# Two of three expert-key tiles beside the value tiles are multiplied as split halves, from a ring of three buffers

## The chip, the core and the metric

The kernel runs on one core of one Trainium2 chip. The metric is the device time of the program in microseconds (us); lower is better. Three runs of the kernel before gave 1677.07, 1669.07 and 1673.76 us, so its median is 1673.76 us. The engines are named as in the profile: PE multiplies matrices (PEld is its weight load), DVE, ACT and POOL work on elements, SP issues transfers.

## The reference

One decoder layer on 512 tokens of width 1024. Three token mixers (forgetting attention, windowed attention, attention to a memory) come first. The change lies in the second half, a product-key layer of 16384 single-neuron experts:

```python
def peer_ffn(h, w_q, keys1, keys2, u, v):
    ...                       # per token: 8 heads x 16 experts by product keys, softmax gates
    def chunk(args):
        h_c, e_c, g_c = args
        a = jnp.einsum('cd,ced->ce', h_c.astype(jnp.float32), u[e_c].astype(jnp.float32))
        act = jax.nn.gelu(a, approximate=False) * g_c
        return jnp.einsum('ce,ced->cd', act, v[e_c].astype(jnp.float32))
```

`u` and `v` are 16384 x 1024 in float32, 64 MB each. A token uses 128 of the 16384 experts.

## The kernel before, in words

The 512 tokens are four blocks of 128. Blocks 0 and 1 take the *row* way: for each of the 128 chosen experts of each token POOL gathers one row of `u` (then of `v`) by an indirect transfer of 128 rows of 4 KB, and DVE multiplies it in (line 819 for `u`, line 828 for `v`). That is 512 row steps; `step()` issues transfers ahead (up to `ahead`, `AHEAD` = 4, `AHEAD + MORE` = 6 for a while) and does one step.

Blocks 2 and 3 (`DENSE`, 256 tokens, `TD`) take the *dense* way: all 16384 experts in 128 tiles of 128.

- `dense_u(k)`: one U tile, 512 KB, comes by SP's queue into a ring of `URING` = 6 buffers (three in the big buffer `hhi`, three in `hlo`). Eight float32 matmuls (line 921, weights: the U tile, moving: `h2f`, the 256 tokens) give the scores; ACT's Gelu puts them into `ga(k)`.
- spreading: `spread(n)` for 64 batches of four tokens turns the gates into a dense layout. Gates of the first 33 tiles are multiplied into `ga` at once, the others go to DRAM (`gd`) and come back later as `gq`, in 512-byte pieces.
- `dense_v(k)`: one V tile, 512 KB. `operands(k)` prepares it: DVE multiplies the gates in from `gq` (line 1036, from k = 33 on), ACT casts the tile to a float32r part `whi` (line 1040), DVE subtracts to get the rest `wlo` (line 125), and `ga(k)` is split likewise into `ah` and `al` (lines 132 and 133). Then `mm3` does three float32r matmuls per piece (lines 137 to 139). Every fourth tile is *whole*: float32 matmuls from a buffer `last`, no split (line 1058).

Splitting a float32 operand into two float32r parts and multiplying three of the four products is `mm3`:

```python
def mm3(ps, l, r, first=True, last=True):
    (lh, ll), (rh, rl) = l, r
    PE.matmul(ps, lh, rh, start=first, stop=False)
    PE.matmul(ps, lh, rl, start=False, stop=False)
    PE.matmul(ps, ll, rh, start=False, stop=last)
```

U runs ahead of V by `LAG` = 57 tiles: U tiles 0 to 57 are done before and during spreading, the other 70 inside the V loop. That loop runs over 128 V tiles; in its turn k stand `operands(k + 1)`, the row steps that are due (about two), the U tile that is due (in 70 of the first 118 turns), and `dense_v(k)`. PE, DVE and POOL execute in the written order (a manual schedule). ACT and SP are put in order by a scheduler. The buffers `raw` (V tiles as they land), `whi` and `wlo` have three slots each; rows may also use `raw` slots while `ahead` is 6. `ah` and `al` have two.

Of the kernel before, what the change touches and what calls it, by code (L numbers as in the profile page):

```python
# [7 lines left out]
F32 = mybir.dt.float32  # L8
F32R = mybir.dt.float32r
# [3 lines left out]
AF = mybir.ActivationFunctionType  # L13
# [3 lines left out]
S, D, NB, KC = 512, 1024, 4, 8  # L17
# [4 lines left out]
NK = 128  # L22
NJ = PH * TOPK
NC = 64
GROUPS = ((0,), (1, 2, 3))
BIG = 3
DENSE = (2, 3)
ND = len(DENSE)
TD = 128 * ND
FIRST_U, COVER, DURING, AFTER = 8, 24, 25, 0  # L30
# [2 lines left out]
BETWEEN, UNWEIGHED, IN_RAW = 12, 14, 0  # L33
LAG = FIRST_U + COVER + DURING + AFTER
GA_LATE = 6
URING = 6
VFAR = 3
GQ_AT, GQ_PARTS = 1, 4
RAW_MORE = 5
STEPS_U = 4  # L40
# [6 lines left out]
WSLOT = 4 * 264  # L47
AHEAD, ROWS_IN, MORE = 4, 5, 2
# [6 lines left out]
def tile_block(ctx: ExitStack, tc: tile.TileContext, t: dict, out: bass.AP):  # L55
    nc = tc.nc
# [12 lines left out]
    def bank(tag):  # L69
        return psum.tile([128, 512], F32, tag=tag, name=tag, bufs=BANKS[tag])  # L70
# [45 lines left out]
    def rest(loaded, pool):  # L116
        raw, hi, n = loaded
        w = raw.shape[1]
        lo = wp.tile([128, WSLOT], F32R, tag="wlo", name="wlo")[:, :w]
        due[0] += pool  # L120
        if due[0] >= 1.0:
            due[0] -= 1.0
            G.tensor_tensor(lo, raw, hi.bitcast(F32), op=OP.subtract)
        else:
            V.tensor_sub(lo, raw, hi.bitcast(F32))  # L125
        return [x.rearrange("p (n w) -> p n w", n=n) for x in (hi, lo)]
# [4 lines left out]
    def split(hi, lo, src):  # L131
        A.copy(hi, src)
        V.tensor_sub(lo, src, hi.bitcast(F32))
# [6 lines that stand above are left out]
# [4 lines left out]
    def wide(tag, nb, dt=F32):  # L144

        slot = big.tile([128, (1 if tag == "mg0" else BIG) * D], dt, tag=tag, name=tag)
        return slot[:, :nb * D]
# [7 lines left out]
    def chunks(x):  # L155

        return [x[:, k] for k in range(x.shape[1])]
# [731 lines left out]
    def ga(k):  # L889
        s = k % (LAG + 1)  # L890
        return soon[:, s] if s <= LAG - GA_LATE else late[0][:, s - (LAG + 1 - GA_LATE)]

    def fetch_u(k):
        if not FIRST_U <= k < NK:
            return
        s = (k - FIRST_U) % URING
        if s % BIG == 0 or not u_ring[s // BIG]:
            if k - FIRST_U < URING:
                u_ring[s // BIG] = by_token(wide(("hhi", "hlo")[s // BIG], BIG))
        u_raw[k] = u_ring[s // BIG][:, s % BIG]  # L900
        nc.sync.dma_start(u_raw[k], t["uT"][k])
# [3 lines left out]
    def fetch_u_to(k):  # L905
        while u_next[0] <= min(k, NK - 1):
            fetch_u(u_next[0])
            u_next[0] += 1

    def dense_u(k):  # L910

        if k < FIRST_U:
            w = load_raw(t["uT"][k], D)[:, :D]
        else:
            fetch_u_to(k + URING - 1)
            w = u_raw.pop(k)
        w = w.rearrange("p (n w) -> p n w", n=KC)
        yield
        ps = bank("mm")
        for dc in range(KC):  # L920
            PE.matmul(ps[:, :TD], w[:, dc], h2f[dc], start=dc == 0, stop=dc == KC - 1)  # L921
            yield
        A.activation(ga(k), ps[:, :TD], AF.Gelu)  # L923
# [48 lines left out]
    def build_sides(n):  # L972
        i, _, ts = tokens(n)
        eT = slots[i]
        o = sp.tile([128, 2, GT, NK], F32, tag="o", name="o", bufs=AHD + 1)
        V.tensor_tensor(o, numbers[:, None, None, :].to_broadcast([128, 2, GT, NK]),
                        eT[:, :2, ts, None].to_broadcast([128, 2, GT, NK]), op=OP.is_equal)
        if n % 4 == 3:
            G.tensor_tensor(o[:, 0], o[:, 0], eT[:, 2, ts, None].to_broadcast([128, GT, NK]), op=OP.mult)
        else:  # L980
            for u in range(GT):
                A.activation(o[:, 0, u], o[:, 0, u], AF.Copy, scale=eT[:, 2, ts.start + u:ts.start + u + 1])
        sides[n] = o
# [35 lines left out]
    def fetch_v(k):  # L1019
        if k < NK:  # L1020
            pool, n = (gp[0], 1) if k % WHOLE == WHOLE - 1 else (wp, None)
            tag = "last" if n else "raw"
            raw = pool.tile([128, D if n else WSLOT], F32, tag=tag, name=tag, **({"bufs": n} if n else {}))
            v_raw[k] = raw[:, :D]
            nc.sync.dma_start(v_raw[k], t["peer_v"][k * NK:(k + 1) * NK])

    def operands(k):

        whole = k % WHOLE == WHOLE - 1
        fetch_v(k + VFAR)  # L1030
        get_gates(k + GK, k % GK - GQ_AT)
        raw, a = v_raw.pop(k), ga(k)
        if k >= KEPT:
            m = gq[k - k % GK][:, :, k % GK]
            g = a.rearrange("p (g t) -> p g t", t=TG)
            V.tensor_mul(g, m, g)
        if whole:
            return whole, [raw], a, a
        hi = wp.tile([128, WSLOT], F32R, tag="whi", name="whi")[:, :D]
        A.copy(hi, raw)  # L1040
        w = [x[:, 0] for x in rest((raw, hi, 1), 0.0)]
        ah = gp[0].tile([128, TD], F32R, tag="ah", name="ah")
        al = gp[0].tile([128, TD], F32R, tag="al", name="al")
        split(ah, al, a)
        return whole, w, ah, al

    def dense_v(k, whole, w, ah, al):
# [14 lines left out]
    NBAT = ND * 128 // GT  # L1062
# [23 lines left out]
    for n in range(AHD, NBAT + AHD):  # L1086
        if n < NBAT:
            build_sides(n)
        credit[0] += STEPS_N
        while credit[0] >= 1.0 and done[0] < known[0]:  # L1090
            credit[0] -= 1.0
            step()
        if (n + 4) % PER == 0 and n + 4 < NBAT:
            turn_block((n + 4) // PER)
        spread(n - AHD)
        for _ in range(STEPS_U):
            if tile_u is None and FIRST_U + COVER + n * DURING // NBAT >= k_u:
                tile_u = dense_u(k_u)
                next(tile_u)
                k_u += 1  # L1100
            elif tile_u is not None and next(tile_u, 1):
                tile_u = None
    for _ in tile_u or ():
        pass
    share[0], ahead[0] = 0.0, AHEAD
    spreading.close()
    gp = [ctx.enter_context(tc.tile_pool(name="gp", bufs=2))]
    while k_u < LAG:
        list(dense_u(k_u))
        k_u += 1  # L1110
    for k in range(VFAR):
        fetch_v(k)
    start, ready = done[0], operands(0)
    for k in range(NK):
        now, ready = ready, operands(k + 1) if k + 1 < NK else None
        while done[0] < min(len(JOBS), start + (len(JOBS) - start) * (k + 1) // (NK - 5)):
            step()
        while k_u < min(NK, LAG + (NK - LAG) * (k + 1) // (NK - 10)):
            list(dense_u(k_u))
            k_u += 1  # L1120
        dense_v(k, *now)
    for b in (0, 1):
        nc.sync.dma_start(out[b * 128:(b + 1) * 128], x1[b])
    for i, b in enumerate(DENSE):
        for hf in range(2):
# [93 lines left out]
```

## Time and profile before

| | |
|---|---|
| runs | 1669.07 to 1677.07 us, median 1673.76 |
| the profiled execution | 1675.4 us; its span, first to last instruction, 1673.5 |
| PE busy | 1583.6 us, 95% |
| DVE / ACT / POOL busy | 1362.9 / 721.9 / 840.7 us |
| memory traffic | 531.80 MB, mean 318 GB/s |
| spreading ends, first V matmul | about 1030 us |
| last V matmul | about 1669 us |

"Busy" on PE runs from the start of a matmul to a modelled end, and matmuls overlap, so PE's pace is read from the starts of matmuls that follow each other. One float32 matmul stands as two records. The DMA share is the time that packets took over 16 engines' time, so it can pass 1 where two packets of an engine overlap.

### The profile page before, as it was taken

To read this page: it belongs to the slowest core of one execution; us is meant where nothing else is said; L and a number is where in the kernel's file an instruction comes from. 1 tells how busy PE (TensorE), PEld (TensorE's weight loads), DVE (VectorE), ACT (ScalarE), POOL (GpSimd) and SP (SyncE) were. 2 spreads that over 40 slices of the span, in tenths; PEclk is the share of its full clock that TensorE was granted. 3 is DMA by queue.
4 is the path that set the end of the run, shared out by engine and by line. 5 is a ranking of instruction groups with operands and counts; after the bars stand their busy time and mean duration, and the time that the engine had idled before them with its cause. 6 is when DMAs were issued, how large, how long until landed. Compare 5 with 4: busy or idle time off the path is not lost.

```text
span 1673.5 us, 25424 instructions
## 1 busy us (share of the span) xinstructions
PE 1583.6 (95%) x8718; PEld 1366.8 (82%) x8718; DVE 1362.9 (81%) x2625; ACT 721.9 (43%) x1586; POOL 840.7 (50%) x664
## 2 busy tenths in 40 slices
PE   6999789999998989988999997999999999999998
PEld 6999679897987979977888996777777777777775
DVE  3777678789988999997999996776678787877786
ACT  6887566556344434544316764222222222222221
POOL 0200251767566556779934543555445555555552
PEclk8999999999998999999999999999999999999999
DMA  6787464898998899767879999999999999999996
GB/s 264 238 260 235 129 195 148 312 360 311 322 336 300 297 337 354 261 207 265 283 260 334 340 345 360 384 378 365 360 383 399 400 397 402 389 401 401 402 386 213
DMA packets 209842, 531.80 MB, mean 318 GB/s; under 512 B 18224, under 2 KB 88112, under 8 KB 209712
## 3 DMA queue, kind: packets, MB, share of 16 engines
q0 software_dynamic: 73728, 268.47, 43.8%
q1 hardware_dynamic: 131376, 249.12, 42.4%
q10 hardware_dynamic: 4608, 12.58, 2.0%
q8 instruction: 69, 1.13, 0.3%
q14 instruction: 61, 0.50, 0.1%
HBM read 515.42 MB, written 14.68 MB: 317 GB/s over the span
## 4 chain that ended last, share of the span: by engine, by line
PE 53%; DMA 15%; DVE 11%; issue 11%; POOL 7%; ACT 3%; SPq 0%; ACTq 0%; POOLq 0%; DVEq 0%
PE mm L921 17%; DMA row<-in_peer_v_dram,eidx 6%; PE mm L138 5%; PE mm L137 5%; PE mm L139 5%; DMA row<-in_peer_u_dram,eidx 5%; POOL row L809 4%; DVE wlo L125 3%; DMA raw<-in_peer_v_dram 2%; DVE scr L819 2%; DVE mg L828 2%; PE sc L994 2%; PE tp L1058 2%; PE sc L1058 2%; PE tp L994 2%
## 5 line engine op out<-in xcount | busy, mean ns | idle before, releaser
L809 POOL DMA_INDIRECT row<-in_peer_u_dram,eidx x256 | 319.7, 1249 | 260.4 <-DVE scr L819 183.2
L809 POOL DMA_INDIRECT row<-in_peer_v_dram,eidx x256 | 326.3, 1275 | 239.4 <-DVE mg L828 175.0
L125 DVE TENSOR_TENSOR wlo<-raw,whi 128x1024 fp32r<-128x1024 f32 (+1 forms) x259 | 327.6, 1266 | 69.1 <-ACT whi L113 37.9
L819 DVE SCALAR_TENSOR_TENSOR scr<-row,h2n 128x1024 bf16<-128x1024 f32 x256 | 313.3, 1224 | 34.7 <-DMA row<-in_peer_u_dram,eidx 31.7
L828 DVE SCALAR_TENSOR_TENSOR mg<-row,acts,mg 128x1024 f32<-128x1024 f32 x222 | 284.3, 1281 | 31.6 <-DMA row<-in_peer_v_dram,eidx 29.1
L113 ACT CAST whi<-raw 128x1024 fp32r<-128x1024 f32 (+1 forms) x172 | 180.2, 1050 | 126.9 <-PE mm L138 57.0
L921 PE MATMUL mm<-h2f,hhi 128*128 128x256 f32 x960 | 222.7, 383 | 2.8 <-ACT ga L923 2.8
L921 PE MATMUL mm<-h2f,hlo 128*128 128x256 f32 x960 | 219.0, 379 | 0.0
L921 PEld LDWEIGHTS mm<-h2f,hlo 128*128 128x128 f32 x960 | 180.2, 190 | 31.7 <-issue 7.4
L921 PEld LDWEIGHTS mm<-h2f,hhi 128*128 128x128 f32 x960 | 181.7, 192 | 28.1 <-ACT ga L923 3.2
L137 PE MATMUL mm<-whi,hhi 128*128 128x256 f32 (+1 forms) x576 | 167.1, 292 | 7.0 <-DVE g L550 1.9
L138 PE MATMUL mm<-wlo,hhi 128*128 128x256 f32 (+1 forms) x576 | 166.1, 289 | 1.0 <-DVE wlo L125 1.0
L139 PE MATMUL mm<-whi,hlo 128*128 128x256 f32 (+1 forms) x576 | 164.2, 287 | 2.4 <-DVE hlo L609 1.6
L923 ACT ACTIVATE ga<-mm 128x256 f32<-128x256 f32 x116 | 44.4, 383 | 275.6 <-PE mm L921 266.2
L1040 ACT CAST whi<-raw 128x1024 fp32r<-128x1024 f32 x96 | 100.2, 1044 | 120.4 <-DMA raw<-in_peer_v_dram 114.5
L137 PEld LDWEIGHTS mm<-whi,hhi 128*128 128x128 f32 x576 | 109.7, 191 | 10.5 <-ACT hhi L603 2.3
L137 PE MATMUL mm<-hhi,whi 128*128 128x384 f32 x320 | 111.3, 348 | 6.3 <-ACT ga L923 3.3
L185 POOL TENSOR_TENSOR rsy<-rsv,mhalf 128x4 f32<-128x4 f32 (+5 forms) x25 | 41.7, 1669 | 145.8 <-DVE rsv L184 145.6
L139 PEld LDWEIGHTS mm<-whi,hlo 128*128 128x128 f32 x576 | 109.8, 191 | 4.5 <-DVE hlo L609 2.0
L138 PEld LDWEIGHTS mm<-wlo,hhi 128*128 128x128 f32 x576 | 110.1, 191 | 3.6 <-DVE wlo L125 1.6
L138 PE MATMUL mm<-hlo,whi 128*128 128x384 f32 x320 | 111.5, 348 | 0.0
L139 PE MATMUL mm<-hhi,wlo 128*128 128x384 f32 x320 | 110.7, 346 | 0.0
(274 smaller groups left out, 3257.8 us busy)
## 6 DMA issues: line engine op xcount, KB each, us to landing
raw<-in_peer_v_dram SPq DMA_DIRECT2D x96, 512.0 KB
hlo<-in_uT_dram SPq DMA_DIRECT2D x60, 512.0 KB
hhi<-in_uT_dram SPq DMA_DIRECT2D x60, 512.0 KB
raw<-in_w_nat_dram SPq DMA_DIRECT2D x40, 512.0 KB
last<-in_peer_v_dram SPq DMA_DIRECT2D x32, 512.0 KB
raw<-in_w_tr_dram SPq DMA_DIRECT2D x48, 256.0 KB
raw<-in_w_o_dram SPq DMA_DIRECT2D x24, 512.0 KB
raw<-in_w_tr_dram SPq DMA_DIRECT2D x24, 512.0 KB
```

The costliest lines, as they stand in the source:

```text
L113: A.copy(hi[:, :n * w], raw[:, :n * w])
L125: V.tensor_sub(lo, raw, hi.bitcast(F32))
L137: PE.matmul(ps, lh, rh, start=first, stop=False)
L138: PE.matmul(ps, lh, rl, start=False, stop=False)
L139: PE.matmul(ps, ll, rh, start=False, stop=last)
L809: G.indirect_dma_start(out=r, out_offset=None, in_=t["peer_" + tab], in_offset=bass.IndirectOffsetOnAxis(ap=eidx[b][:, j:j + 1], axis=0))
L819: V.scalar_tensor_tensor(scr, r, 1.0, h2n[b], op0=OP.mult, op1=OP.mult, accum_out=acts[b][:, c]))
L828: V.scalar_tensor_tensor(x1[b], r, acts[b][:, c], x1[b], op0=OP.mult, op1=OP.add))
L921: PE.matmul(ps[:, :TD], w[:, dc], h2f[dc], start=dc == 0, stop=dc == KC - 1)
L994: PE.matmul(ps[:, u], o[:, 1, u], o[:, 0, u], start=True, stop=True)
L1040: A.copy(hi, raw)
L1058: PE.matmul(acc[i, hf], al[:, tok], w[0][:, d], start=k == 0, stop=k == NK - 1)
```

## The change

Five things are done together.

1. U tiles with k of at least 57 that are not multiples of 3 (47 of the 70 in the V loop) are split: ACT casts the tile into a `whi` slot, DVE subtracts into a `wlo` slot, and `mm3` does 24 float32r matmuls of 256 columns instead of eight float32 ones. The 256 tokens are split once, into `h2s`.
2. `h2s` takes the big buffer `hlo` and `mg0`. So the U ring shrinks from six buffers to the three of `hhi` once k reaches 57, and the result of block 0, which lay in `mg0`, is stored before V begins instead of at the end of the program.
3. In a turn the U tile's parts are prepared before the row steps, as before, but its matmuls stand behind `dense_v(k)` and no longer ahead of it.
4. V's first three tiles are asked for five batches before spreading's last one. For that, rows stop using `raw` slots (`ahead` back to 4) twelve batches before.
5. In `operands`, ACT's cast to `ah` is issued ahead of the cast to `whi`, and DVE's `al` stays behind `wlo`.

```diff
-URING = 6
+URING, URING_V = 6, 3
+U_WHOLE = 3
+PLAIN_ROWS, V_EARLY = 12, 5
@@ fetch_u
-        s = (k - FIRST_U) % URING
+        s = (k - FIRST_U) % URING if k < LAG else (k - LAG + 1) % URING_V
@@ dense_u
-            fetch_u_to(k + URING - 1)
+            fetch_u_to(k + URING_V - 1 if k >= LAG else min(k + URING - 1, LAG + 1))
             w = u_raw.pop(k)
+        if k >= LAG and k % U_WHOLE:
+            hi = wp.tile([128, WSLOT], F32R, tag="whi", name="whi")[:, :D]
+            A.copy(hi, w)
+            w = [x[:, 0].rearrange("p (n w) -> p n w", n=KC) for x in rest((w, hi, 1), 0.0)]
+            yield
+            ps = bank("mm")
+            for dc in range(KC):
+                mm3(ps[:, :TD], [x[:, dc] for x in w], [x[dc] for x in h2s], dc == 0, dc == KC - 1)
+            A.activation(ga(k), ps[:, :TD], AF.Gelu)
+            return
@@ operands
+        ah = gp[0].tile([128, TD], F32R, tag="ah", name="ah")
+        al = gp[0].tile([128, TD], F32R, tag="al", name="al")
+        A.copy(ah, a)
         hi = wp.tile([128, WSLOT], F32R, tag="whi", name="whi")[:, :D]
         A.copy(hi, raw)
         w = [x[:, 0] for x in rest((raw, hi, 1), 0.0)]
-        split(ah, al, a)
+        V.tensor_sub(al, a, ah.bitcast(F32))
@@ spreading
+        if n == NBAT - PLAIN_ROWS:
+            ahead[0] = AHEAD
+        if n == NBAT - V_EARLY:
+            for k in range(VFAR):
+                fetch_v(k)
@@ the V loop
-    for k in range(VFAR):
-        fetch_v(k)
     start, ready = done[0], operands(0)
+    nc.sync.dma_start(out[0:128], x1[0])
+    h2s = [t.rearrange("p (k t) -> p k t", t=TD) for t in (wide("hlo", BIG, F32R), wide("mg0", 1, F32R))]
+    h2s = chunks(h2s[0][:, :KC]), chunks(h2s[0][:, KC:]) + chunks(h2s[1])
+    for dc in range(KC):
+        split(h2s[0][dc], h2s[1][dc], h2f[dc])
     for k in range(NK):
         now, ready = ready, operands(k + 1) if k + 1 < NK else None
+        us = []
+        while k_u < min(NK, LAG + (NK - LAG) * (k + 1) // (NK - 10)):
+            us.append(dense_u(k_u))
+            next(us[-1])
+            k_u += 1
         while done[0] < min(len(JOBS), start + (len(JOBS) - start) * (k + 1) // (NK - 5)):
             step()
-        while k_u < min(NK, LAG + (NK - LAG) * (k + 1) // (NK - 10)):
-            list(dense_u(k_u))
-            k_u += 1
         dense_v(k, *now)
-    for b in (0, 1):
+        for u in us:
+            list(u)
+    for b in (1,):
```

How it moves instructions is shown at three places. First PE, after the first three V tiles (`sc` and `tp` are the sums, `mm` the U scores; `x8` counts equal instructions). Before, a whole U tile follows, then the whole V tile 3 (`last`), then another U tile:

```order
L139 MATMUL tp<-whi,al 128x512
L921 MATMUL mm<-h2f,hhi 128x256 x8
L1058 MATMUL sc<-last,ga 128x512 x2
L1058 MATMUL tp<-last,ga 128x512 x2
L921 MATMUL mm<-h2f,hlo 128x256 x8
L137 MATMUL sc<-whi,ah 128x512
```

Now V tile 3 comes first and the U tile behind it is a split one (lines 139 to 141 are `mm3` now; its eight groups of three are cut to two here):

```order
L141 MATMUL tp<-whi,al 128x512
L1071 MATMUL sc<-last,ga 128x512 x2
L1071 MATMUL tp<-last,ga 128x512 x2
L139 MATMUL mm<-hlo,whi 128x256
L140 MATMUL mm<-hlo,whi 128x256
L141 MATMUL mm<-hlo,wlo 128x256
L139 MATMUL mm<-hlo,whi 128x256
L140 MATMUL mm<-hlo,whi 128x256
L141 MATMUL mm<-hlo,wlo 128x256
```

A split tile is 24 matmuls with 24 weight loads, where eight float32 matmuls stood, and U moves behind V in its turn. Second DVE, at the head of the V loop. Before, from the last spreading product (line 997) on:

```order
L997 TENSOR_TENSOR ga<-tp,ga 128x32x4
L125 TENSOR_TENSOR wlo<-raw,whi 128x1024
L133 TENSOR_TENSOR al<-ga,ah 128x256
L125 TENSOR_TENSOR wlo<-raw,whi 128x1024
L133 TENSOR_TENSOR al<-ga,ah 128x256
L819 SCALAR_TENSOR_TENSOR scr,acts_176<-row,h2n 128x1024 x2
L125 TENSOR_TENSOR wlo<-raw,whi 128x1024
L133 TENSOR_TENSOR al<-ga,ah 128x256
L819 SCALAR_TENSOR_TENSOR scr,acts_176<-row,h2n 128x1024 x4
```

And now:

```order
L1009 TENSOR_TENSOR ga<-tp,ga 128x32x4
L127 TENSOR_TENSOR wlo<-raw,whi 128x1024
L1057 TENSOR_TENSOR al<-ga,ah 128x256
L135 TENSOR_TENSOR hlo<-h2f,hlo 128x256 x4
L135 TENSOR_TENSOR mg_11143<-h2f,hlo 128x256 x4
L127 TENSOR_TENSOR wlo<-raw,whi 128x1024
L1057 TENSOR_TENSOR al<-ga,ah 128x256
L821 SCALAR_TENSOR_TENSOR scr,acts_176<-row,h2n 128x1024 x2
L127 TENSOR_TENSOR wlo<-raw,whi 128x1024
L1057 TENSOR_TENSOR al<-ga,ah 128x256
L821 SCALAR_TENSOR_TENSOR scr,acts_176<-row,h2n 128x1024 x4
```

The eight subtractions for `h2s` stand between the first and the second V tile; from V tile 4 on one `wlo<-hhi` per split U tile is added in front of the row steps. Third SP's queue around the end of spreading. Before:

```order
L1123 DMA out_dram<-mg_2214 128x1024
L901 DMA hhi<-in_uT_dram 128x1024 x2
L901 DMA hlo<-in_uT_dram 128x1024 x3
L1025 DMA raw<-in_peer_v_dram 128x1024 x2
L901 DMA hhi<-in_uT_dram 128x1024
L1025 DMA last<-in_peer_v_dram 128x1024
L1017 DMA gq<-gd_9315 128x4x128 x2
L1017 DMA gq<-gd_9316 128x4x128
L1017 DMA gq<-gd_9315 128x4x128
L1025 DMA raw<-in_peer_v_dram 128x1024
```

And now:

```order
L1037 DMA raw<-in_peer_v_dram 128x1024
L903 DMA hlo<-in_uT_dram 128x1024
L903 DMA hhi<-in_uT_dram 128x1024
L1131 DMA out_dram<-mg_2214 128x1024
L903 DMA hhi<-in_uT_dram 128x1024
L1037 DMA raw<-in_peer_v_dram 128x1024
L903 DMA hhi<-in_uT_dram 128x1024
L1037 DMA raw<-in_peer_v_dram 128x1024
L903 DMA hhi<-in_uT_dram 128x1024
L1037 DMA last<-in_peer_v_dram 128x1024
L1029 DMA gq<-gd_9315 128x4x128 x2
```

V's tiles 0, 1 and 2 now stand between U tiles 53 to 58, ahead of the first gate pieces `gq`; before, V tile 2 stood behind four of them. The store of block 0 was put early by the scheduler in the kernel before too.

More of the change, by code (lines that the diff above doesn't have):

```diff
@@ L895, in fetch_u @@
             return
-        s = (k - FIRST_U) % URING
-        if s % BIG == 0 or not u_ring[s // BIG]:
+        s = (k - FIRST_U) % URING if k < LAG else (k - LAG + 1) % URING_V
+        if s % BIG == 0:
             if k - FIRST_U < URING:
@@ L1041, in operands @@
         w = [x[:, 0] for x in rest((raw, hi, 1), 0.0)]
-        ah = gp[0].tile([128, TD], F32R, tag="ah", name="ah")
-        al = gp[0].tile([128, TD], F32R, tag="al", name="al")
-        split(ah, al, a)
+        V.tensor_sub(al, a, ah.bitcast(F32))
         return whole, w, ah, al
@@ L1104, in tile_block @@
         pass
-    share[0], ahead[0] = 0.0, AHEAD
+    share[0] = 0.0
     spreading.close()
@@ L1110, in tile_block @@
         k_u += 1
-    for k in range(VFAR):
-        fetch_v(k)
     start, ready = done[0], operands(0)
+    assert start >= 2 * NJ
+    nc.sync.dma_start(out[0:128], x1[0])
[3 more added lines that the diff above has]
+        split(h2s[0][dc], h2s[1][dc], h2f[dc])
     for k in range(NK):
         now, ready = ready, operands(k + 1) if k + 1 < NK else None
+        us = []
[3 more added lines that the diff above has]
+            k_u += 1
         while done[0] < min(len(JOBS), start + (len(JOBS) - start) * (k + 1) // (NK - 5)):
             step()
-        while k_u < min(NK, LAG + (NK - LAG) * (k + 1) // (NK - 10)):
-            list(dense_u(k_u))
-            k_u += 1
         dense_v(k, *now)
-    for b in (0, 1):
+        for u in us:
+            list(u)
+    for b in (1,):
         nc.sync.dma_start(out[b * 128:(b + 1) * 128], x1[b])
```

## The prediction, made before the changed kernel ran

> **What bounds the kernel now.** I read the windows first, because the change touches the V loop alone. The rows below cut that part of the span: the passage from spreading to V, V until the read-back of gates becomes regular, V with that read-back, and the tail. Columns: length, busy time of PE, PEld, DVE, ACT, POOL, granted clock, DMA share, GB/s.
>
> ```profile
> core 0: us, PE busy (x) PEld busy (x) DVE busy (x) ACT busy (x) POOL busy (x), PEclk, DMA share, GB/s
> 1027.00:1052.00 25.00, 15.38 (x53) 10.95 (x52) 11.85 (x18) 6.48 (x12) 5.50 (x4) 0.80 1.05 360
> 1052.00:1100.00 48.00, 48.00 (x195) 36.59 (x194) 37.15 (x59) 12.76 (x21) 26.76 (x20) 1.00 1.01 394
> 1100.00:1240.00 140.00, 140.00 (x579) 109.11 (x578) 96.96 (x156) 34.41 (x58) 65.81 (x53) 1.00 0.98 368
> 1240.00:1620.00 380.00, 378.28 (x1554) 293.07 (x1553) 298.69 (x380) 94.36 (x160) 209.01 (x152) 1.00 1.03 398
> 1620.00:1673.50 53.50, 47.26 (x171) 32.74 (x169) 38.87 (x49) 10.47 (x17) 16.21 (x11) 0.97 0.68 247
> ```
>
> From 1052 to 1620 us PE has no hole, and the 16 DMA engines have none either. So two things are at their limit at once, and the question is which of them holds when PE's work shrinks. Next I read the timeline of PE, to see that a busy PE is also a PE at its pace: one whole U tile, and the last of the V tile behind it.
>
> ```profile
> 1430.92 3.62 PE L921 MATMUL mm<-h2f,hlo 128*128 128x256 f32 x16
> 1434.18 0.58 PE L137 MATMUL sc<-whi,ah 128*128 128x512 f32 x1
> 1434.60 0.39 PE L138 MATMUL sc<-wlo,ah 128*128 128x512 f32 x1
> ...
> 1436.91 0.39 PE L139 MATMUL tp<-whi,al 128*128 128x512 f32 x1
> ```
>
> The ten steps from 1434.60 to 1436.91 are 0.231 us each; a V tile of twelve is 2.8 us. The chain puts the U tile at 3.45 us:
>
> ```profile
> 1431.08 3.45 PE mm L921 x16
> ```
>
> PE at its pace thus fills the loop. The DMA side is told by the highest rate that any long piece shows:
>
> ```profile
> 1536.00:1556.00 20.00, 20.00 (x83) 15.43 (x82) 15.17 (x18) 5.12 (x9) 10.48 (x9) 1.00 1.03 414
> ```
>
> 414 GB/s over 20 us, against a mean of 398 in the long stretch with the same share of 1.03. The lower mean goes with the 512-byte gate pieces, which that stretch has more of. I take the stretch from 1240 to 1620 as held by the DMA engines as much as by PE. From 1100 to 1240, at 368 GB/s, there are 46 GB/s to spare.
>
> **The split tile.** The kernel already runs float32r matmuls of 256 columns with a weight load each, in the mixers:
>
> ```profile
> 300.50 0.28 PE L137 MATMUL mm<-whi,hhi 128*128 128x256 f32 x1
> ...
> 302.28 0.28 PE L137 MATMUL mm<-whi,hhi 128*128 128x256 f32 x1
> ```
>
> These are 15 steps in 1.78 us, 0.119 us each, so 24 take 2.85 us where the whole tile takes 3.45: 0.60 us less, 47 times, 28.2 us of PE. Their weight loads are on record too:
>
> ```profile
> L137 PEld LDWEIGHTS mm<-whi,hhi 128*128 128x128 f32 x576 | 109.7, 191 | 10.5 <-ACT hhi L603 2.3
> ```
>
> A load shows 191 ns and yet matmuls start every 119 ns, so loads overlap with matmuls and with each other. The Trainium skill ("TensorE: Matmul & The Clock Gate", Part 3, "The mechanism") says that a weight load overlaps a running matmul only where the row group differs, which here it does not. By that rule the 24 loads would lie bare between the matmuls; the trace does not agree, since 119 is under 191.
>
> The added preparation is one cast and one subtraction per split tile; and here are DVE's other pieces of a turn:
>
> ```profile
> L1040 ACT CAST whi<-raw 128x1024 fp32r<-128x1024 f32 x96 | 100.2, 1044 | 120.4 <-DMA raw<-in_peer_v_dram 114.5
> L125 DVE TENSOR_TENSOR wlo<-raw,whi 128x1024 fp32r<-128x1024 f32 x93 | 114.3, 1229 | 14.3 <-ACT whi L1040 12.3 <-issue 2.0
> L133 DVE TENSOR_TENSOR al<-ga,ah 128x256 fp32r<-128x256 f32 x84 | 35.3, 420 | 66.4 <-ACT ah L132 66.4
> L828 DVE SCALAR_TENSOR_TENSOR mg<-row,acts,mg 128x1024 f32<-128x1024 f32 x128 | 164.1, 1282 | 27.6 <-DMA row<-in_peer_v_dram,eidx 25.7 <-DVE mg L828 0.2
> L819 DVE SCALAR_TENSOR_TENSOR scr<-row,h2n 128x1024 bf16<-128x1024 f32 x114 | 139.4, 1223 | 21.5 <-DMA row<-in_peer_u_dram,eidx 19.6
> ```
>
> ACT gets 47 x 1.04 = 49 us more in 568, and is a quarter busy: hidden. DVE gets 47 x 1.23 = 58 us. By time the stretch 1240 to 1620 holds 47 x 380/568 = 31.5 of the tiles, so DVE goes there from 299 to 338 of 380 us, 89%: not the bound, but its 66 us of waiting for `ah`, which is running ahead of PE, is the slack that goes. Queued behind the new subtraction on DVE are the two row steps, and POOL's next row transfer waits for these.
>
> What is not free is the buffers. `whi` and `wlo` still have three slots, now for V and U. In the built program 18 of the 47 tiles get a `whi` slot whose last reader stands only one V tile (2.8 us) ahead of the tile's own matmuls; cast and subtraction take 1.04 + 1.23 = 2.27 us in that gap if ACT and DVE stand ready, and DVE may be in a row step of 1.2 to 1.3 us. So such a tile makes PE wait between 0 and 1.3 + 2.27 us. The nearest row, `wlo` late by 14.3 us over 93 tiles, is near the lower end; I take 0.7 us, half a row step.
>
> **The passage to V.** Views: the chain, SP's queue and PE's timeline around 1040 us.
>
> ```profile
> 1024.32 7.26 DMA raw<-in_peer_v_dram
> 1036.07 8.67 DMA raw<-in_peer_v_dram
> 1044.76 1.05 ACT whi L1040
> 1045.84 1.24 DVE wlo L125
> ```
> ```profile
> 1022.98 1.67 SPq L1025 DMA_DIRECT2D raw<-in_peer_v_dram  x2
> 1027.65 8.31 SPq L1017 DMA_DIRECT2D gq<-gd  x4
> 1036.07 2.31 SPq L1025 DMA_DIRECT2D raw<-in_peer_v_dram  x1
> ```
> ```profile
> 1045.86 0.80 PE L137 MATMUL sc<-whi,ah 128*128 128x512 f32 x1 [8.30 <-ACT whi L1040]
> 1051.98 3.71 PE L921 MATMUL mm<-h2f,hhi 128*128 128x256 f32 x16
> ```
>
> V tile 2 is asked for at 1036.07, behind four gate pieces on SP, and PE stands for 8.30 us; then the tile takes 6.1 us instead of 2.8, since the clock had fallen (0.80 in the first window). That is 8.3 + 3.3 = 11.6 us at most. With the three tiles asked for ahead of spreading's end this goes; late next is DVE: eight subtractions for `h2s` of 0.42 us, 3.4 us, stand between V tiles 0 and 1, and ACT has eight casts of like size at the end of spreading. The worst is that both lie bare and nothing is gained, +3. I take 7 us gained, 11.6 less the 3.4 and a little. The three tiles also sit in SP's queue among U tiles 53 to 58, where a tile that waits for a `raw` slot holds up the U tiles behind it; U tile 57 is multiplied last in spreading, so there are some tens of us to spare, and I cost that at nothing. The early store of block 0 was at this place already: nothing. The shorter row lookahead over twelve batches: nothing, DVE being the busy engine there.
>
> **The sum**, against the profiled execution's 1675.4 us (1673.5 of span, 1.9 around it; 1.6 above the median of the runs):
>
> - passage: -7 (bounds -11.6 and +3);
> - 1052 to 1240, DMA not at its limit: 15.5 split tiles x 0.60 = -9.3 of PE, six of them with the short cover x 0.7 = +4.2, so -5 (bounds -9.3 and +12, six times 3.6);
> - 1240 to 1620: PE gives up 31.5 x 0.60 = 19 us, but 380 us x 398 GB/s = 151 MB must come, and at 414 GB/s that is 365 us. The share is 1.03 already, which speaks for no gain: -2 (bounds -15 and, with waits that DMA slack can no longer cover, +15). The waits for slots vanish in these 19 us;
> - tail: 0. Rows and V alone; the one store of 512 KB that left was not on the chain.
>
> Sum -14: 1661 us, and 1660 against the median. About 0.5% (8.4 us) is what a measurement of this kernel can tell from no change; under 1665.4 is faster, over 1682.1 slower.
>
> **Rivals.**
>
> *PE's whole gain arrives.* If the DMA engines follow a faster PE, the time is 1675.4 - 7 - 28 + 2 = 1642. For it: PE had no stall in the long stretch, so transfers did keep up, and pieces of 414 GB/s exist. Against it: a share of 1.03 in every window from 1240 on. The Trainium skill ("DMA: Bandwidth & Descriptors", section "Where 436 GB/s comes from") puts the ceiling at 435 GB/s; by that the 151 MB need 348 us and PE would decide, with this rival's time. No window here reaches it.
>
> *Parts come late.* The ring of three and the shared slots make PE wait for the split parts, w us per tile on the mean. Each tile then gains 0.60 - w, and the passage gives 7. It is slower by over 0.5% once 47 x (w - 0.60) passes 7 + 8.4, that is w over 0.93. If the 18 short-cover tiles wait their full 2.27 us and the other 29 wait 0.6, w is 1.24 and the time 1675.4 - 7 + 30 = 1698; more likely halfway, 1686. For it: DVE at 89% in strict order; the lookahead of U down from five tiles to two. Against it: only 14 us of such waits before. Part of this: weight loads that lie bare, 24 x (0.19 + 0.12) = 7.4 us a tile, +184 us in all; the mixers' rows exclude that nearly, and I give it 0.01.
>
> *Nothing moves.* The DMA engines are full at 1027 to 1052 as well (1.05) and at 1100 (0.98 to 1.01), so early V tiles only displace rows and gates, and what PE saves turns into waits for transfers: 1672.
>
> **Chances.** The forecast 0.47, with a range of its own of 1652 to 1668; PE's whole gain 0.17; nothing moves 0.20; parts late 0.16. Of the forecast 0.40 lies under 1665.4 and 0.07 above; so faster is 0.40 + 0.17 = 0.57, same 0.07 + 0.20 + 0.02 (late parts that only eat the gain) = 0.29, slower 0.14. A range from 1642 to 1687 leaves out about half of the first rival and over half of the slow one, some 0.18.
>
> **What would show it.** The passage: no PE idle over 2 us between V tiles 1 and 2, and a clock of 1.00 there. The tile: `mm` from `whi` at 0.12 us a step, 2.85 us. DVE busy up by about 58 us, near 89% in the gated stretch. The gated stretch as long as before with GB/s near 400, and PE now with idle time whose releaser is a transfer, or ACT's cast behind one. Wrong would be: 415 GB/s or more held over that stretch (first rival), or PE's idle time released by `wlo` on DVE with a DMA share under 1.00 (late parts).

## The result, and the profile after

The changed kernel takes 1700.04 us (median of six runs, 1694.65 to 1702.12), the kernel before 1674.82 (six runs). The ratio is 1.0138, with a 95% interval of 1.0112 to 1.0164: slower, where faster was forecast. The profiled execution took 1702.12 us, with a span of 1700.4.

The windows of the changed kernel, cut as in the prediction but without the tail (length, busy time of PE, PEld, DVE, ACT, POOL, granted clock, DMA share, GB/s):

```profile
core 0: us, PE busy (x) PEld busy (x) DVE busy (x) ACT busy (x) POOL busy (x), PEclk, DMA share, GB/s
1027.00:1052.00 25.00, 24.26 (x129) 20.57 (x129) 21.83 (x40) 13.00 (x38) 11.26 (x8) 1.00 0.82 283
1052.00:1100.00 48.00, 37.72 (x181) 29.97 (x180) 32.14 (x48) 14.39 (x21) 21.45 (x17) 0.89 1.00 375
1100.00:1240.00 140.00, 137.15 (x672) 109.61 (x671) 117.18 (x179) 45.73 (x70) 82.59 (x60) 0.99 1.00 386
1240.00:1620.00 380.00, 352.60 (x1723) 280.38 (x1722) 314.78 (x392) 117.49 (x182) 198.28 (x142) 0.98 1.01 382
```

PE, which had next to no hole from 1052 to 1620 us, now has 27 us of them in the long stretch alone (380 less 352.60), and GB/s there fell from 398 to 382. The waits of PE from 1030 us on say at what it stands (columns: what waits, for what; us in total, times, longest):

```profile
PE mm L141 <- DVE wlo L127: 33.4, 18, 3.1
PE mm L139 <- ACT whi L921: 6.1, 1, 6.1
PE sc L139 <- ACT ah L1053: 6.1, 5, 1.4
```

`mm` at line 141 is the third matmul of a split U tile, the first that reads `wlo`; it waits for DVE's subtraction. The split tile itself does what was forecast, here its steps on PE's timeline:

```profile
1058.83 0.28 PE L139 MATMUL mm<-hlo,whi 128*128 128x256 f32 x1
1058.95 0.28 PE L140 MATMUL mm<-hlo,whi 128*128 128x256 f32 x1
...
1061.17 0.28 PE L141 MATMUL mm<-hlo,wlo 128*128 128x256 f32 x1
```

20 steps in 2.34 us, 0.117 us each. (The rule on bare weight loads cited in the prediction from the Trainium skill, "TensorE: Matmul & The Clock Gate", Part 3, would have shown as 0.31 us, an estimate from the rows of the prediction, 0.19 for a load and 0.12 for a step; this trace does not agree with it either.)

To see where the time is, I take the V part, from the first V matmul to the end of the span, and split it by the starts of PE's matmuls: each has its step at pace (0.231, 0.119, 0.216 and 0.430 us by kind, from rows without stalls), and what is over is a stall (over 0.45 us) or a slow step. The V part is these three and some 5 us behind the last matmul.

| | spreading begins | V part | PE's work at pace | stalls | slow steps |
|---|---|---|---|---|---|
| before | 880.8 | 643.2 | 617.3 | 13.9 | 7.0 |
| before, second trace (e9) | 885.4 | 640.7 | 617.3 | 12.3 | 6.0 |
| changed | 892.5 | 658.8 | 589.3 | 49.1 | 15.9 |
| changed, second trace (e5) | 886.8 | 661.3 | 589.3 | 49.2 | 18.2 |

On the mean of the two traces of each kernel PE's work fell by 28.0 us, the stalls rose by 36 and the slow steps by 10. That makes the V part 18 us longer (15.6 and 20.6 by the rows taken in pairs). The other 7 of the 25 us lie ahead of V: up to spreading the order of every engine is the same, spreading began anywhere from 877.7 to 892.5 us in the 18 traces of this study, and from there to the first V matmul it is 147 to 150 us in all of them.

One stall in full. PE's timeline, changed kernel; the `sc` row is the start of a V tile, the `mm` rows are the split U tile behind it:

```profile
1315.69 0.50 PE L139 MATMUL sc<-whi,ah 128*128 128x512 f32 x1 [1.44 <-ACT ah L1053]
...
1318.57 0.28 PE L139 MATMUL mm<-hlo,whi 128*128 128x256 f32 x1
1318.69 0.28 PE L140 MATMUL mm<-hlo,whi 128*128 128x256 f32 x1
1321.81 0.39 PE L141 MATMUL mm<-hlo,wlo 128*128 128x256 f32 x1 [2.84 <-DVE wlo L127]
...
1323.67 0.41 PE L139 MATMUL mm<-hlo,whi 128*128 128x256 f32 x1
1323.88 0.41 PE L140 MATMUL mm<-mg,whi 128*128 128x256 f32 x1
```

PE stands 2.84 us for `wlo`, and 1.3 us after it has resumed the steps go from 0.118 to 0.21 us. The granted clock in these microseconds (columns as in the windows above):

```profile
1321.81:1323.15 1.34, 1.34 (x11) 1.34 (x12) 1.30 (x3) 0.00 (x0) 0.00 (x0) 1.00 0.67 269
1323.15:1326.56 3.41, 3.41 (x16) 3.22 (x16) 3.41 (x5) 0.90 (x1) 2.98 (x2) 0.50 0.80 237
```

The clock is granted at 0.50 for 3.41 us, then at 1.00 again. DVE in the same microseconds:

```profile
1308.02 0.42 DVE L1048 TENSOR_TENSOR late<-gq,late 128x256 f32<-128x256 f32 x1
1308.36 1.27 DVE L127 TENSOR_TENSOR wlo<-raw,whi 128x1024 fp32r<-128x1024 f32 x1
1315.67 0.42 DVE L1057 TENSOR_TENSOR al<-late,ah 128x256 fp32r<-128x256 f32 x1 [6.04 <-ACT ah L1053]
1316.01 1.22 DVE L821 SCALAR_TENSOR_TENSOR scr<-row,h2n 128x1024 bf16<-128x1024 f32 x1
...
1318.76 1.22 DVE L127 TENSOR_TENSOR wlo<-raw,whi 128x1024 fp32r<-128x1024 f32 x1
1320.19 0.43 DVE L1057 TENSOR_TENSOR al<-late,ah 128x256 fp32r<-128x256 f32 x1 [0.21 <-ACT ah L1053]
1320.54 1.22 DVE L127 TENSOR_TENSOR wlo<-hhi,whi 128x1024 fp32r<-128x1024 f32 x1
```

The U tile's `wlo` (1320.54) starts after PE wants it. DVE was idle for 6.04 us in front of `al`, for want of `ah`, and then did everything that stood ahead in its written order. And ACT:

```profile
1311.49 0.38 ACT L935 ACTIVATE ga<-mm 128x256 f32<-128x256 f32 x1 [5.84 <-PE mm L933]
1314.29 1.04 ACT L921 CAST whi<-hhi 128x1024 fp32r<-128x1024 f32 x1 [2.41 <-PE tp L141]
1315.24 0.40 ACT L1053 CAST ah<-late 128x256 fp32r<-128x256 f32 x1
```

`ah`, whose input DVE had ready at 1308.44 (L1048), stands behind a Gelu that waits for PE, and then behind the cast of a U tile, and that cast waits until PE has done with its `whi` slot (`tp` L141, the last matmul of a V tile). ACT's order is a scheduler's, and it put the U tile's cast first. So a slot that comes late holds not only its own tile but, through ACT and `al`, the whole of DVE.

The ten longest stalls for `wlo` (2.6 to 3.1 us) are not all of this make. The first, at 1058.61, and the 6.1 us for `whi` at 1070.31 follow tiles and rows that landed late, and e1 below keeps both. In two of the other nine, at 1291.81 and 1503.48, it is not a U tile's cast that stands ahead of `ah` but a V tile's, which waits 5.5 and 5.6 us for its slot:

```profile
1288.81 1.04 ACT L1055 CAST whi<-raw 128x1024 fp32r<-128x1024 f32 x1 [5.50 <-PE tp L141]
1289.76 0.40 ACT L1053 CAST ah<-ga 128x256 fp32r<-128x256 f32 x1
```

### The profile page after: what moved, and what is told of

It reads as the page before. It is cut to its first block, busy times and chain, and to the rows that moved or that the text cites. A ratio compares the mean times of both kernels' runs of the same rounds, so it can differ in the third digit from the quotient of the medians.

```text
span 1700.4 us, 26421 instructions
## 1 busy us (share of the span) xinstructions
PE 1572.1 (92%) x9094; PEld 1371.0 (81%) x9094; DVE 1417.3 (83%) x2680; ACT 767.5 (45%) x1641; POOL 854.4 (50%) x664
## 5 line engine op out<-in xcount | busy, mean ns | idle before, releaser
L811 POOL DMA_INDIRECT row<-in_peer_u_dram,eidx x256 | 331.4, 1294 | 254.7 <-DVE scr L821 169.1
L821 DVE SCALAR_TENSOR_TENSOR scr<-row,h2n 128x1024 bf16<-128x1024 f32 x256 | 313.5, 1225 | 37.6 <-DMA row<-in_peer_u_dram,eidx 33.4
L933 PE MATMUL mm<-h2f,hhi 128*128 128x256 f32 x784 | 181.2, 381 | 3.7 <-ACT ga L935 3.7
L933 PEld LDWEIGHTS mm<-h2f,hhi 128*128 128x128 f32 x784 | 146.8, 191 | 26.3 <-ACT ga L935 4.5
L141 PE MATMUL mm<-whi,hlo 128*128 128x256 f32 (+1 forms) x576 | 163.8, 286 | 2.8 <-DVE hlo L611 1.6
L140 PE MATMUL mm<-hlo,whi 128*128 128x384 f32 (+1 forms) x508 | 166.1, 327 | 0.0
L141 PE MATMUL mm<-hlo,wlo 128*128 128x256 f32 x376 | 112.2, 298 | 33.4 <-DVE wlo L127 33.4
L139 PE MATMUL mm<-hlo,whi 128*128 128x256 f32 x376 | 114.5, 304 | 6.2 <-ACT whi L921 6.1
L187 POOL TENSOR_TENSOR rsy<-rsv,mhalf 128x4 f32<-128x4 f32 (+5 forms) x25 | 41.2, 1650 | 144.3 <-DVE rsv L186 144.0
L141 PEld LDWEIGHTS mm<-whi,hlo 128*128 128x128 f32 x576 | 109.5, 191 | 5.0 <-DVE hlo L611 2.0
L141 PE MATMUL mm<-hhi,wlo 128*128 128x384 f32 x320 | 110.8, 346 | 0.0
L141 PEld LDWEIGHTS mm<-hlo,wlo 128*128 128x128 f32 x376 | 75.9, 202 | 37.2 <-DVE wlo L127 37.2
```

Source lines behind the costliest of these rows:

```text
L187: G.tensor_tensor(y, v, mhalf[:, :n], op=OP.pow)
L811: G.indirect_dma_start(out=r, out_offset=None, in_=t["peer_" + tab], in_offset=bass.IndirectOffsetOnAxis(ap=eidx[b][:, j:j + 1], axis=0))
L821: V.scalar_tensor_tensor(scr, r, 1.0, h2n[b], op0=OP.mult, op1=OP.mult, accum_out=acts[b][:, c]))
```

## The experiments

Theories: **A**, ACT's order, as just read; **S**, the slots' short cover by itself, the prediction's term (the cover of a split U tile is PE's work between the last reader of its slot and the tile's own matmuls); **B**, DVE's written order, which puts the U tile's `wlo` behind 2.07 us of the next V tile's pieces; **C** and **D**, the transfer engines, as cause of the stalls (C) or as what holds the V part once they are gone (D).

**e1: ACT's order alone.** A U tile's cast is held until the `ah` of its turn is out, and `ah` is written behind the V tile's cast; the run does not tell the two apart.

```diff
-        A.copy(ah, a)
         hi = wp.tile(...)
         A.copy(hi, raw)
+        last_ah[0] = A.copy(ah, a)
@@ dense_u
-            A.copy(hi, w)
+            with tc.issue_after(last_ah[0].ins): A.copy(hi, w)
```

> The changed kernel, with ACT's cast of a U tile issued only after the cast `ah` of the same turn (ACT's order alone; DVE, PE and POOL as in the changed kernel). Theory A (ACT's order: the U tile's cast waits for a whi slot and holds `ah` behind it, DVE's `al` waits for `ah` up to 6 us, and the U tile's `wlo` comes late by that): the 33.4 us in which PE waits for `wlo` and the 6.1 us for `ah` fall below 10 us in all, and with the clock that falls after each stall the time drops by 35 to 45 us, to 1655 to 1665. Theory B (DVE's written order: `wlo` of the U tile stands behind mul, wlo and al of the next V tile, 2.07 us, whatever ACT does): most of the 33.4 us stays, time 1690 to 1700. Theory C (ring of three, transfers late): no change, 1700.

Measured 1668.85 us (ratio to before 0.9960, 0.9937 to 0.9983), 31 less than the changed kernel; V part 634.5. PE's waits:

```profile
PE mm L141 <- DVE wlo L127: 13.9, 16, 3.8
PE mm L139 <- ACT whi L921: 7.5, 6, 4.0
PE sc L139 <- ACT ah L1055: 1.5, 2, 0.8
```

The waits fell from 46 to 23 us, not below 10, and the time fell by somewhat less than the 35 to 45 us that A gave; B and C, which had it stay at 1690 or more, are out. From 1100 us on, the stalls of 2.8 us for `wlo` are gone, and the eleven that are left are all alike:

```profile
1408.06 0.39 PE L141 MATMUL mm<-hlo,wlo 128*128 128x256 f32 x1 [0.76 <-DVE wlo L127]
```

What comes before it, on ACT and on DVE:

```profile
1405.39 0.41 ACT L1055 CAST ah<-ga 128x256 fp32r<-128x256 f32 x1 [3.42 <-DVE ga L1048]
1405.70 2.18 ACT L921 CAST whi<-hhi 128x1024 fp32r<-128x1024 f32 x2
1402.34 2.60 DVE L830 SCALAR_TENSOR_TENSOR mg<-row,acts,mg 128x1024 f32<-128x1024 f32 x2
1404.86 0.41 DVE L1048 TENSOR_TENSOR ga<-gq,ga 128x256 f32<-128x256 f32 x1
1406.78 1.23 DVE L127 TENSOR_TENSOR wlo<-hhi,whi 128x1024 fp32r<-128x1024 f32 x1
```

In all eleven the U tile's cast follows `ah` without a pause, and `ah` has waited 3.3 to 5.2 us for DVE's product of line 1048, in front of which DVE does row steps. So it is not a slot that the cast waits for here, and the 0.76 us are not the price of short cover; that they lie next to the prediction's 0.7 is chance. Six of the eleven are tiles with k mod 12 = 1 or 10, which are not among the 18 of short cover. B is not the cause of the 2.8 us, since DVE's order is untouched; but with the cast behind `ah`, DVE's written order sets what is left.

**e2: the U tile's parts first.** The block that prepares the U tile's parts is moved ahead of `operands(k + 1)`.

```diff
-        now, ready = ready, operands(k + 1) if k + 1 < NK else None
         us = []
         while k_u < ...:
             ...
+        now, ready = ready, operands(k + 1) if k + 1 < NK else None
```

> The changed kernel, with the preparation of the U tile (cast and subtraction) written ahead of that of the next V tile, on DVE and for ACT's planner. Theory B (DVE's written order): each of the 14 stalls of some 2.5 us loses up to 2.07 us, with their clock loss 25 to 35 us: 1665 to 1675. Theory A (ACT's order): ACT still meets casts that wait for a slot ahead of `ah`; DVE is held as long as before, stalls of PE on `wlo` or on `ah` stay at 20 us or more, and the time stays above 1680. Theory C: 1700.

Measured 1676.55 (1.0018, 0.9996 to 1.0039), V part 643.7. The time lies between the two ranges, and the waits have moved, not gone:

```profile
PE sc L139 <- ACT ah L1053: 17.1, 13, 1.9
PE mm L141 <- DVE wlo L127: 10.1, 12, 2.2
```

V's matmuls now wait for `ah`. The run can't decide for B, since the edit also gave every split U tile 5.6 us of cover or more in the built program (18 had 2.8), and e1 did better without it. My bound for A (above 1680) was too high.

**e3: no U tile split.**

```diff
-U_WHOLE = 3
+U_WHOLE = 1
```

> The changed kernel with no U tile split (all 70 by float32 matmuls); ring of three, U behind V, early V tiles and the moved store stay. If the parts of the split tiles cause the loss (A or B): the stalls on `wlo` go (35 us, and some 9 us of slow clock), and 47 x 0.60 = 28 us of PE come back: 1700 - 44 + 28 = 1684, or 1663 if the first 1040 us take as long as in the kernel before (1674.8 less the 12 us gained in the passage to V). If the ring of three or full transfer engines cause it (C): PE waits for transfers, and the time stays at 1695 or more.

Measured 1673.19 (0.9984, 0.9964 to 1.0004), V part 638.3. No stall on parts, and 27 us less than the changed kernel with the same ring of three and U behind V, so these are not what costs 25 us (C falls as the cause). One stall is left where the passage's gain should be, at 1063.78 us:

```profile
1063.78 0.80 PE L139 MATMUL sc<-whi,ah 128*128 128x512 f32 x1 [6.77 <-ACT whi L1055]
```

Its cast had itself waited for the landing of a `raw` tile. The changed kernel has the same 6 us at 1070.31 (`whi` L921, queued on ACT behind such a cast). So of the 12 us gained up to V tile 2 (it ends 9.9 us after V's start, before 21.9) half goes into the next tile that lands late, and by V tile 10 nothing is left in the changed kernel (62.2 us, before 62.8).

**e4: early V tiles alone**, on the kernel before.

```diff
+        if n == NBAT - PLAIN_ROWS: ahead[0] = AHEAD
+        if n == NBAT - V_EARLY:
+            for k in range(VFAR): fetch_v(k)
```

> The kernel before with only V's first three tiles asked for five batches before spreading's end and the rows kept out of their slots for twelve batches. The traces of before and after show 12 us less between the start of V tile 0 and the end of V tile 2. If that is a gain by itself: 1674.8 - 12 = 1663. If it is only work moved, because the transfer engines are full there: 1672 to 1675. The first V matmul came at 1030 us before and at 1042 after; if the shorter lookahead of rows or the early tiles delay spreading it will come at 1035 or later here, and if that was chance, near 1030.

Measured 1667.67 (0.9958, 0.9939 to 0.9978): 6.2 us less, where the prediction's term was 7. V part 634.9. V tile 10 ends about 56 us after V's start, so here half of the 12 us stays. V began at 1035.6, but spreading had begun 5.8 us later too, and the program is the same up to there: that is the first part's variation, not the edit.

**e5 and e9: both kernels again**, unaltered.

> The changed kernel once more, unaltered, to see how long its first part and its V part take in a second profiled execution. The first V matmul came at 1030.3 (before), 1041.6 (changed), 1037.0, 1030.4, 1034.0 and 1035.6 us in the traces so far, all but the first with the same program up to there. If that is variation from run to run, this one falls somewhere from 1030 to 1042, and the V part, from the first V matmul to the end of the span, is again near 658.8 us. If the changed kernel is late there by its program, it comes at 1040 or later again.

> The kernel before once more, for a second profiled execution. Spreading began at 880.8 us in its first trace, and at 880.1 to 892.5 in the nine traces of kernels that share its program up to there. If the first part varies by chance, it begins anywhere from 880 to 893 here. The V part (first V matmul to the end of the span) was 643.2 us; near that again if the program sets it, and 16 to 18 below the changed kernel's 658.8 and 661.3.

e5: 1700.55 (1.0143, 1.0117 to 1.0168). e9: 1674.18 (1.0002, 0.9979 to 1.0026). Their V parts are in the table above. The long stalls of e5 are those of the first trace, nearly place by place (2.85, 2.80, 2.84 us ...): they are made by the order, not by chance.

**e6: the 18 tiles of short cover whole**, ACT's order left.

```diff
-        if k >= LAG and k % U_WHOLE:
+        if k >= LAG and k % U_WHOLE and k % 12 not in (2, 4, 11):
```

> The changed kernel with the 18 tiles of short cover (a whi slot freed 2.8 us of PE work ahead of their matmuls: k mod 12 = 2, 4 or 11) multiplied whole; 29 tiles stay split, all with 6 us of cover or more; ACT's order is left to the planner. Theory S (the slots' short cover is what costs): waits for `wlo` and `ah` fall below 5 us, the V part takes 617 - 29 x 0.60 + 14 = 614 us or little more, the time is 1648 to 1655. Theory A alone (casts of U ahead of `ah` on ACT, whatever the cover): the waits fall only by the tiles' share, to some 25 us, and the time is 1670 or more.

Measured 1682.12 (1.0030, 1.0006 to 1.0054), V part 644.4. S falls here: no split tile has much under 6 us of cover, and yet PE waits 17.1 us, ten times, for `wlo`. The changed kernel says the same: of its nine long stalls behind the first, four fall on tiles with k mod 12 = 1, which have some 9.5 us of cover, and five on the six tiles with k mod 12 = 4; of the twelve short-cover tiles with k mod 12 = 2 or 11 only one waits 0.3 us or more, the one behind the late tile at 1070.31. That A makes all ten waits of e6 is not shown; some casts ahead of `ah` wait for transfers there.

**e7 and e8: U's matmuls one V tile later**, e8 with ACT's order of e1 as well.

```diff
-        us = []
+        us, last_us = [], us
@@
         dense_v(k, *now)
-        for u in us:
+        for u in last_us if k < NK - 1 else last_us + us:
             list(u)
```

> The changed kernel with the matmuls of a turn's U tile put one V tile later on PE (behind the next turn's V tile); the parts are prepared where they were. In the built program every split tile now has 5.6 us or more of PE work between the last reader of its slot and its own matmuls, where 18 had 2.8. Theory S (short cover): waits for `wlo` vanish but for a few us, V part 589 + 15 to 20 = 605 to 610 us, time 1637 to 1650. Theory A (ACT's order, which is not changed here): the late `ah` stays and shows as waits of V's matmuls, 15 us or more as in the run with U's parts first (21 us there); time 1660 or more.

> The run before with ACT's cast of a U tile issued only behind the `ah` of its turn as well, so both suspected costs are taken away. If short cover and ACT's order are the whole loss: PE's waits in the V part under 10 us, V part 600 to 608 us, time 1635 to 1648. If the transfer engines or DVE hold the loop at that pace: time 1655 or more, with PE idle released by a transfer or by `mul` and `wlo` of V tiles, and DMA share above 1.02 or DVE at 90% or more in the stretch.

e7: 1674.80 (0.9994, 0.9976 to 1.0013), 21.7 us of waits for `ah`, as A said; S had 1637 to 1650. e8: 1668.77 (0.9949, 0.9928 to 0.9970), no better than e1, though no wait of `mm` is left. Of e8's waits the largest is for a transfer:

```profile
PE sc L1071 <- DMA last<-in_peer_v_dram: 7.9, 2, 4.4
PE sc L139 <- ACT ah L1055: 5.0, 5, 2.0
```

V parts: e1 634.5, e4 634.9, e8 636.7, with 589, 617 and 589 us of PE's work. That three kernels end at the same length points to a limit that they share.

**e10, e11, e12: without the read-back of gates.** In `get_gates`, groups after the first are not read; `gq` of the first group stands in for them. These kernels leave the right gates out and do not compute the layer; the engines' work is the same, and 44 transfers of 256 KB in 512-byte pieces are gone. e10 is e8 with it, e11 is e4, e12 is the changed kernel.

```diff
@@ get_gates
+        if k > KEPT:
+            gq[k] = gq[KEPT]
+            return
         if part == 0:
```

> The kernel with U one V tile later and ACT's cast behind `ah`, but without the read-back of gates after its first group (44 transfers of 256 KB in 512-byte pieces are left out, and the first group's gates are used in their place; engines do the same work). Its V part was 636.7 us, 589 of PE work. Theory D (with the waits for parts gone, the transfer engines hold the V part at some 635 us): the V part falls to 595 to 612 us and the time to 1628 to 1645. Theory E (DVE's written order or ACT holds it): it stays within 8 us, 1660 or more.

> The kernel before with early V tiles alone, again without the read-back of gates after the first group. Its V part was 634.9 us, 617.5 of PE work. If PE holds it at 617 and some 13 us of stalls and slow clock: 1655 to 1667, a gain of 12 us at most. If the transfer engines hold it: as much gain as in the kernel with U later, 25 us or more, which PE's own work excludes, so the V part stops at 620 us.

> The changed kernel without the read-back of gates after the first group. Theory S and A (its loss comes from short cover and ACT's order): PE still waits 25 us or more for `wlo` of U tiles, V part 645 us or more, time 1680 to 1698. Theory C/D (its loss comes from full transfer engines): the waits go, V part 610 us, time 1640 to 1650.

| | with the read-back | without | V part without |
|---|---|---|---|
| early V alone (e4, e11) | 1667.67 | 1659.65 | 626.9 |
| changed kernel (e5, e12) | 1700.55 | 1664.28 | 633.2 |
| both cures (e8, e10) | 1668.77 | 1637.53 | 606.6 |

Theory D holds: with the transfers relieved the cured kernel goes 22 us below e11, near the 28 us of PE's work that the split saves; with them it is no faster. e12 came out between its two ranges: PE still waits 23.2 us for `wlo`, a little under the 25 that S and A gave, but 36 us are gained. So the read-back lengthens the changed kernel's stalls as well; it does not make them all. The windows from 1240 to 1620 us, e8 and then e10:

```profile
1240.00:1620.00 380.00, 366.87 (x1771) 284.05 (x1769) 327.55 (x398) 123.48 (x189) 202.22 (x150) 0.98 1.03 395
```
```profile
1240.00:1620.00 380.00, 378.36 (x1864) 297.89 (x1863) 347.95 (x421) 129.71 (x197) 209.16 (x155) 1.00 1.00 388
```

PE goes from 367 to 378 of 380 us, DVE to 348 (92%): DVE was not at its limit in e8. The DMA share does not tell the two apart: it is 1.00 in e10 too, where PE is at its pace. And "the transfers" is more than the engines: the 36 gate issues of this stretch also held SP's queue, with V tiles behind them, for 51 us in e8 and 16 us in e15 below. Whether the engines or SP's queue is the limit, these runs do not separate.

**e13 and e14: one cure each, without the read-back**, so that the transfers do not mask it: ACT's order (e1) in e13, U one tile later (e7) in e14.

> The changed kernel with ACT's cast of a U tile behind the `ah` of its turn, and without the read-back of gates after its first group (as in the three runs before: the first group's gates are used in its place). Without the read-back the changed kernel took 1664.3 us and the one with both cures 1637.5, so 26.8 us are to be divided. If ACT's order is the larger cause: 1640 to 1648. If short cover is: 1653 to 1662. If each is enough by itself to bring the stall: near 1660 here and in the next run.

> The changed kernel with U's matmuls one V tile later, ACT's order left to the planner, and again without the read-back of gates after the first group. If short cover is the larger cause of the 26.8 us: 1640 to 1648. If ACT's order is: 1653 to 1662, with waits of V's matmuls for `ah` of 15 us or more.

e13: 1647.78 (0.9841, 0.9820 to 0.9863). e14: 1664.27 (0.9934, 0.9912 to 0.9956), the same as with no cure (1664.28). Their largest waits, e13 and then e14:

```profile
PE mm L141 <- DVE wlo L127: 9.2, 11, 3.4
```
```profile
PE sc L139 <- ACT ah L1056: 21.0, 16, 1.5
```

Of the 26.8 us that both cures bring, ACT's order alone brings 16.5; U one tile later alone brings nothing, the wait only moves from `wlo` to `ah`; on top of ACT's order it brings the other 10.3. It gives the split parts 2.8 us more whatever makes them late, so the 10.3 are not a measure of short slots.

**e15 and e16: gates in pieces twice as long.** `TG` 32 for 16, so 1024-byte packets; staging in three slots. e15 is e8 with it, e16 is e4.

```diff
-TG = 16
+TG = 32
-SPILT = (128 - KEPT) // 2
+SPILT = (128 - KEPT) // 3
-            ... for tag in ("whi", "wlo")]
+            ... for tag in (("whi", "whi", "wlo") if t0 // TG % 2 else ("wlo", "wlo", "whi"))]
```

> The kernel with both cures (1668.8 us) and gates kept in pieces twice as long: 32 tokens instead of 16, so the read-back comes in 1024-byte packets, half as many, with the same bytes; in spreading the staging takes three slots instead of two and ACT copies in three pieces instead of two. A 512-byte packet took 29 ns and a 4096-byte one 159 to 166, so 1024 bytes should take some 45 ns, and the read-back 24,576 x 29 / 16 = 44.5 us less 34.6, about 10 us. If the transfer engines hold the V part: 1656 to 1663. If they do not: 1667 to 1671; slower if the third copy on ACT holds up spreading.

> The kernel before with early V tiles (1667.7 us) and the same longer pieces of gates. Without any read-back after the first group it gained 8 us, since PE's 617 us hold it then; with half the packets it should gain 2 to 5: 1662 to 1666. If the transfer engines alone hold it, 10: 1658.

e15: 1659.58 (0.9906, 0.9881 to 0.9930), V part 629.2. e16: 1666.99 (0.9947, 0.9922 to 0.9973), V part 634.9, as without. The counts of packets, e8 from 1240 to 1620 us and e15 from 1240 to 1610:

```profile
DMA packets 57538, 150.01 MB, mean 395 GB/s; under 512 B 4844, under 2 KB 23276, under 8 KB 57513
```
```profile
DMA packets 48200, 149.52 MB, mean 404 GB/s; under 512 B 4842, under 2 KB 14058, under 8 KB 48175
```

Nearly the same bytes in nine thousand packets fewer and ten microseconds less. The kernel with the split gains 9 us by the medians (7 by the ratios to the kernel before), as expected; the one without gains 1 (2), where 2 to 5 were expected. e15 is the fastest version here that computes the layer: early V tiles, split parts, U one V tile later, ACT's cast behind `ah`, longer pieces.

## Why the prediction was wrong

- **The split tile, -28.2 us of PE: right.** 28.0, at the steps of rows without stalls.
- **The passage, -7: right by itself, lost in the changed kernel.** e4 measured 6.2 less. The changed kernel gains 12 us up to V tile 2, with the clock at 1.00 as said, and has given all of it back by V tile 10.
- **ACT, "a quarter busy: hidden": the step that failed.** ACT was costed by its load, and 49 us more are nothing for an engine 31% busy with them. But a cast that waits for a slot blocks what is queued behind it, and behind it stood `ah`, then `al`, then all of DVE. With that one order changed, e1 is 31 us faster. ACT's order in the built program could be read before the run; what stands ahead of the prediction shows it for PE, DVE and SP only. The prediction did ask what is queued behind the new subtraction on DVE, and not what is queued behind the new cast.
- **The short cover, 0.7 us on 18 tiles: wrong in size and in mechanism.** It measured 33.4 us over 18 waits, ten of them 2.6 to 3.1, and they do not follow the cover. The 0.76 per stall in e1 is another wait.
- **The stretch from 1052 to 1240, -5: near.** From the end of V tile 10 to the end of V tile 40 it is 147.4 us, before 150.6; in e1 144.3.
- **"The waits for slots vanish in these 19 us" (the slack of the transfer engines): wrong.** Seven of the ten long stalls lie in that stretch, from the end of V tile 40 to that of V tile 126 it is 441.7 us where it was 422.0, and the transfers did not run ahead: 382 GB/s against 398, at a share of 1.01. During some stalls the transfers fell too (a share of 0.58 from 1318.69 to 1321.81), during others not (1.02 from 1397.00 to 1399.80); how much of the loss comes about in this way is not shown.
- **The clock was left out.** At six of the ten long stalls the granted clock falls to 0.50 for 3.41 us, from 0.6 us before PE resumes to 1.3 us after; slow steps are some 10 us more in all (9 and 12 by the rows in pairs).
- **The gated stretch held by transfers: right,** for a kernel without the 2.8 us stalls. In e1 V tiles 40 to 126 take 420.2 us where they took 422.0: the split's gain does not arrive there, as the -2 said. That the read-back is behind it, e10 shows; engines or SP's queue stays open.
- **The rival, parts late,** had its sum right, though not ACT's order as the reason. Waits of 45.6 us over 47 tiles are 0.97 us, with 9 us of slow steps 1.16: by its formula 1675.4 - 7 + 47 x 0.56 = 1695, against 1700 measured. It got 0.16 because "only 14 us of such waits before" was read as evidence; those were waits in a kernel whose ACT has no cast of a U tile. Its mark, idle time released by `wlo` on DVE, was seen; the DMA share did not go under 1.00 with it.
- **DVE +58 us: 54** (1362.9 to 1417.3). It reached 83% of the gated stretch, not 89%, because it waited itself.

Left open: the 7 us of the difference that lie ahead of V. Two traces of each kernel differ there by 5 and 6 us themselves, and kernels with the same program up to V began spreading as early as 879.3; whether the changed kernel is late there more often than by chance, these traces can't tell.

## What to carry to other kernels

When a new instruction is put on a lightly loaded engine, do not cost it by load: ask what it waits for and what is queued behind it, above all where a scheduler sets that engine's order and a strict order follows downstream. An engine that is a quarter busy can still set the pace. And before counting PE's saving, ask whether another resource is at its limit in the same stretch: here two cures were worth 27 us together without the read-back, and the second showed nothing until it was gone.

## What the runs showed of the hardware

After some stalls of PE of 2.6 to 2.9 us, and not after others, its granted clock is 0.50 for 3.41 us: at six of the ten long stalls of the first trace of the changed kernel. The steps then go from 0.118 to 0.21 us, and from 0.231 to 0.43 for 512 columns. A shorter stall is no protection: in the kernel before, the clock falls at 1656.33, 1.3 us after a stall of 1.62 us. What decides it, these traces do not show. A 512-byte packet took 29 ns, a 1024-byte one 47 and a 4096-byte one 163 to 168 (means from 1240 to 1620 us in before, changed, e8, e10 and e15), so 17.7, 21.8 and about 25 bytes per ns on an engine. The Trainium skill ("DMA: Bandwidth & Descriptors", section "Specifications") gives 512 bytes and more as enough for line rate. Here it is about 0.7 of the rate at 4096 bytes, and in the kernel with both cures, which the transfers hold, 1024 bytes were worth 7 to 9 us.
